# A hybrid SSD, pooling and top-4-of-32 MoE block: another order of the experts, and down weights stored in 8 KB runs

## Chip, cores and metric

One core of a Trainium2 chip. The metric is the device time of one launch in microseconds (us); the kernel before takes 1842.26 us (median of 3 runs, 1841.16 to 1846.85).

## What is computed

The reference is one decoder block on 512 tokens of width 1024: a Mamba-2 branch and a pooling branch, merged by gates, then a mixture of experts, all in float32. The change is in the experts alone:

```python
logits = xt @ w_router + b_router
top_val, top_idx = lax.top_k(logits, 4)          # 4 of 32 experts for each token
gate = softmax(top_val)
# every expert gets its own tokens, padded to a block of rows:
gu = xblk @ w_gu[e] + b_gu[e]                    # 1024 -> 2048
glu, lin = split(gu, 2)
glu = minimum(glu, 7.0); lin = clip(lin, -7.0, 7.0)
act = glu * sigmoid(1.702 * glu) * (lin + 1.0)
y = act @ w_down[e] + b_down[e]                  # 1024 -> 1024
# y * gate is added to the token's row
```

An expert's weights are 12 MB (8 MB up, 4 MB down), so 32 experts read 384 MB.

## The kernel before

**Ranks and blocks.** The kernel counts each expert's tokens on the chip and sorts the experts by that count. `ROOM` gives each rank a fixed number of slots: rank 0 (expert 0, always taken first) 128, ranks 1 to 15 64 (a *half* block), ranks 16 to 30 72 to 128 (a *whole* block), and rank 31, the largest expert, 192: a whole block and a half one with the same weights. `order_of_ranks` (L62) writes the order of the ranks down as a table; `order[u]` is the rank of the u-th unit of work, and `big` is the place of rank 31. In the table `s` draws the next half rank, `f` the next whole one, and `None` stands for rank 31. Before, the order is 0, 1, 2, then 16, 3, 17, 4, 18, 5, 19, 6, 20, 7, 31, 8, 21, 9, 22, 10, 23, 11, 24, 12, 25, 13, 26, 27, 28, 29, 30, 14, 15.

**A unit on TensorE.** The loop over u (L1358) does `up(u)`, then `down(u - 1)`, so that the activation of unit u runs beside the down projection of the unit before it. `up` starts with the bias rows (`bias_rows`: L1107 for a whole block, L1104 for a half one, output `mm`) and takes 8 pieces of 1 MB; `down` starts with bias rows too (output `ss`) and takes 4 pieces. The starts of these bias matmuls mark the stretches of the program in the trace. A whole block's weights are split in two halves of float32r parts by ScalarE (`wh`, L117) and VectorE (`wl`, L118), 1024 columns at a time and into two buffers, and each product is three matmuls (L1118 to L1120). A half block takes its weights straight from the loaded tile in float32 (L1113), without a split.

**Beside it.** `acts` (act_rows, L1154 to L1156, and act_turn, L1164 or L1167) makes the activation of unit u in hooks inside `down(u - 1)`. `turned(u + 1)` transposes and normalizes the next unit's tokens (L1066, L1074) in the same `down`. `send` scales the result (L1178) and GpSimd adds it to the output in DRAM.

**Weight loads.** All weight loads stand in one queue, SP's (`fetch`, L771), in the order in which they are used: 8 up pieces of unit u, then 4 down pieces of unit u - 1. They go round a ring of tiles of 1 MB (7 that come back, and 4 more after unit 0: 11 in all); a load waits until its tile's last reader is done.

Of the kernel before, what the change touches and what calls it, by code (L numbers as in the profile page):

```python
# [20 lines left out]
P = 128  # L21
D = 1024
# [4 lines left out]
NE = 32  # L27
# [33 lines left out]

def order_of_ranks():  # L62
    s, f = iter(range(FIXED, FIXED + SMALL)), iter(range(FIXED + SMALL, NE - 1))
    kinds = [s, s] + [f, s] * 5 + [None, s] + [f, s] * 5 + [f] * 5 + [s, s]
    return list(range(FIXED)) + [next(k) if k else NE - 1 for k in kinds]


# [1 line left out]
def hybrid_block(ctx: ExitStack, tc: tile.TileContext, cst, cols, rows, xt, xf, wad0, wada, bada,  # L69
                 wx, wz, wdt, wu, wg, wso, wpl, wpo, wo, wr, ball, wgu, wdn, out):  # L70
    nc = tc.nc
    V, S, G, TE, SP = nc.vector, nc.scalar, nc.gpsimd, nc.tensor, nc.sync
# [9 lines left out]
    def T_(tag, cols_, dt=F32, parts=P):  # L82
        if tag in shared:
            o = shared[tag]
            return Z[0:parts, o:o + cols_]
        uid[0] += 1
        return sb.tile([parts, cols_], dt, tag=tag, name=f"{tag}_{uid[0]}")
# [655 lines left out]
    def weights(e):  # L743
        def of(w, lo_, hi_):
            return w[e, lo_:hi_, :] if isinstance(e, int) else w[bass.ds(e, 1), lo_:hi_, :].squeeze(0)

        return dict(wu=lambda k: of(wgu, k * P, (k + 1) * P), got={},
                    wd=lambda c: of(wdn, c * 256, (c + 1) * 256).rearrange("(k p) d -> p k d", p=P))

    order = order_of_ranks()  # L750
    big = order.index(NE - 1)
    tab, wts, rk = {}, {}, {}

    def weights_of(u):
        if u not in wts:
            wts[u] = weights(order[u] if u < FIXED else
                             SP.value_load(rk["eidi"][0:1, order[u]:order[u] + 1], min_val=0, max_val=NE - 1))
        return wts[u]
# [6 lines left out]
    def fetch(w, kind, k, t=None):  # L765
        if t is None:
            t = ring.pop(0)
            if t not in ("S7", "r3", "S3"):
                ring.append(t)
        r = T_(t, 2048)  # L770
        SP.dma_start(r if kind == "wu" else r.rearrange("p (k d) -> p k d", k=2), w[kind](k))  # L771
        return r

    def eload(w, kind, k):
        return w["got"].pop((kind, k), None) or fetch(w, kind, k)
# [46 lines left out]
    def prefetch(i0, i1):  # L822
        w = weights_of(0)
        for k in range(i0, i1):
            w["got"]["wu", k] = fetch(w, "wu", k)

    def fetch_down(c0, c1):
        w = weights_of(0)
        for c in range(c0, c1):
            w["got"]["wd", c] = fetch(w, "wd", c, kept[c])  # L830
# [400 lines left out]
    def tabled(u):  # L1231
        ev = SP.value_load(tab["eui"][0:1, u], min_val=0, max_val=NE - 1)
        ec, ub, eo, pu, gvu, gvf = (T_(n, c, d) for n, c, d in (
            ("ec", 2, F32), ("ub", 1, F32), ("eo", NE, F32), ("pu", 4, F32), ("gvu", 12, BF16), ("gvf", 12, F32)))
        V.tensor_copy(ec[:, 0:1], tab["euf"][:, u])
        V.tensor_copy(ec[:, 1:2], tab["ruf"][:, u])
        V.tensor_copy(ub, tab["ubase"][:, u])
        V.tensor_scalar(eo, i32c, ec[:, 1:2], None, op0=ALU.is_equal)
        gvt = T_("q16", 512)
        pv = gvt[:, 0:P].rearrange("p (b e) -> p b e", b=NB)  # L1240
        tt(pv, rk["pos"], eo.unsqueeze(1).to_broadcast([P, NB, NE]), ALU.mult)
        V.tensor_reduce(pu, pv, axis=AX.X, op=ALU.add)
        V.tensor_scalar(pu, pu, ub, None, op0=ALU.subtract)
        gvx = gvt[:, P:P + 384].rearrange("p (b c e) -> p b c e", b=NB, c=3)
        for b in range(NB):
            tt(gvx[:, b], GVv[:, b].rearrange("p e c -> p c e"), eo.unsqueeze(1).to_broadcast([P, 3, NE]), ALU.mult)
        V.tensor_reduce(gvf.rearrange("p (b c) -> p b c", c=3), gvx, axis=AX.X, op=ALU.add)
        V.tensor_copy(gvu, gvf)
        eT = T_("eT", 2, F32R)
        sel_halves(eT, ec[:, 0:1])  # L1250
        return dict(pos=lambda b: pu[:, b:b + 1], gv=lambda b: gvu[:, b * 3:(b + 1) * 3], sel=dict(cols=eT), **weights(ev))
# [12 lines left out]
    def sel_of(u):  # L1264
        if u < FIXED:
            return dict(cols=sel0[:, 2 * u:2 * u + 2])
        return dict(cols=sels[u % 2], wide=wides[u % 2])
# [90 lines left out]
    for u in range(NE + 1):  # L1358
        hooks = {}
        if u < NE:  # L1360
            w, sel = weights_of(u), sel_of(u)
# [73 lines left out]
    with tc.For_i(0, nov, 1) as i:  # L1435
        lastp.clear()
        w = tabled(bass.ds(i, 1))
# [20 lines left out]
def _consts():  # L1458
    c = np.zeros((P, C_ALL), np.float32)
    i = np.arange(P)  # L1460
    c[:, C_ID:C_ID + P] = np.eye(P)
    c[:, C_TRI:C_TRI + P] = i[:, None] <= i[None, :]
    c[:, C_STRI:C_STRI + P] = i[:, None] < i[None, :]
    c[:, C_IOTA:C_IOTA + P + 1] = np.arange(P + 1)[None, :]
    c[:, C_E:C_E + 32] = (i[:, None] % 32) == np.arange(32)[None, :]
    for g in range(4):
        c[:, C_RC + g * 16:C_RC + (g + 1) * 16] = 1.0 / np.minimum(np.arange(16) + 1, 2 << g)
    c[:, C_P], c[:, C_NP] = i, -i
    c[:, C_P5] = i + 512
    c[:, C_PM:C_PM + 2] = (i % 32)[:, None]  # L1470
    c[:, C_B:C_B + 4] = np.arange(4) * P - 512
    key = np.arange(NE)
    key[:FIXED] -= 40000 * (FIXED - key[:FIXED])
    c[:, C_KR:C_KR + NE] = key
    c[:, C_KC] = key[i % 32]
    c[:, C_HM] = i < 64
    c[:, C_H] = i >= 64
    c[:, C_BD:C_BD + 4] = (i // 32)[:, None] == np.arange(4)
    c[:, C_CAP:C_CAP + NE] = [room(r) for r in range(NE)]
    return c  # L1480


def _layout(i):
    A = np.ascontiguousarray

    def tiles(w):
        return w.reshape(KD, P, w.shape[1] // P, P).transpose(2, 1, 0, 3)

    def pairs(t):
        return t.reshape(-1, 2, P, 1024).transpose(0, 2, 1, 3).reshape(-1, P, 2048)  # L1490

    def halves(w):
        n = w.shape[1] // 512
        return w.reshape(2, 4, P, n, 512).transpose(3, 0, 2, 1, 4).reshape(n, 2, P, 2048)

    x, w_in = i["x"][0], i["w_in"][0]
    fcol = lambda v: v.reshape(-1, P).T
    cols = np.concatenate([
        i["conv_w"][0].reshape(4, 24, P).transpose(2, 1, 0).reshape(P, 96), fcol(i["conv_b"][0]),
        fcol(i["ssd_norm_w"][0]), fcol(i["pool_scale"][0]), fcol(i["norm_mix_w"][0]), fcol(i["c"][0]),  # L1500
        fcol(i["norm_ffn_w"][0]), fcol(np.repeat(i["d_skip"][0], 64)),
        fcol(i["norm_final_w"]), fcol(i["b_ada"][0][:2048]).reshape(P, 2, 4, 2).transpose(0, 2, 1, 3).reshape(P, 16)], axis=1)
    rows = np.concatenate([i["a_log"][0], i["dt_bias"][0], i["b_router"][0]])
    order = [t for g in range(4) for t in (16 + g, 20 + g, 4 * g, 4 * g + 1, 4 * g + 2, 4 * g + 3)]
    d = dict(
        cst=_consts(), cols=A(cols), rows=rows,
        xt=A(x), xf=A(x.T.reshape(2, 4, P, T).transpose(0, 2, 1, 3).reshape(2, P, 2048)),
        wad0=A(i["w_ada"][0][:, :2048].reshape(2, 4, P, 2, 4, 256).transpose(4, 0, 2, 1, 3, 5).reshape(4, 2, P, 2048)), wada=A(halves(i["w_ada"][0][:, 2048:])), bada=A(i["b_ada"][0].reshape(12, 512)),
        wx=A(pairs(tiles(w_in[:, 2048:5120])[order])),
        wz=A(pairs(tiles(w_in[:, 0:2048]))),  # L1510
        wdt=A(w_in[:, 5120:5152].reshape(KD, P, NH).transpose(1, 0, 2).reshape(P, 256)),
        wu=A(pairs(tiles(w_in[:, 5152:6176]))),
        wg=A(pairs(tiles(w_in[:, 6176:8224]))),
        wso=A(i["w_ssd_out"][0].reshape(4, 4, P, 2, 4, P).transpose(0, 3, 2, 4, 1, 5).reshape(8, P, 2048)),
        wpl=A(i["w_pool"][0].reshape(4, 2, P, 256).transpose(2, 0, 1, 3).reshape(P, 2048)),
        wpo=A(pairs(tiles(i["w_pool_out"][0]))),
        wo=A(halves(i["w_out"][0]).reshape(4, P, 2048)),
        wr=A(i["w_router"][0].reshape(KD, P, NE).transpose(1, 0, 2).reshape(P, 256)),
        ball=A(np.concatenate([i["b_gu"][0], i["b_down"][0]], axis=1).reshape(NE, 3, 2, 512).transpose(2, 0, 1, 3).reshape(2, NE, 1536)),
        wgu=A(i["w_gu"][0]), wdn=A(i["w_down"][0]))  # L1520
    return d


# [17 lines left out]
```

## Time and profile before

| | us |
|---|---|
| median of 3 runs | 1842.26 (1841.16 to 1846.85) |
| the profiled execution | 1837.33 |
| its span, first to last instruction | 1835.5 |

TensorE's matmuls are busy 1754.0 us (96% of the span), VectorE 1210.0 (66%), ScalarE 947.1 (52%), GpSimd 237.5 (13%). The experts fill the second part of the span, from about 709 us on. The chain that ended last is of no use here: it is cut after its last instruction. So the kernel is read by stretches: which engine's idle time ends with whom, and how long a unit takes beside which neighbours.

### The profile page before, as it was taken

How to read it: one execution, taken by the hardware profiler on the slowest of the kernel's cores; microseconds unless marked ns; L12 is line 12 of the kernel's file. 1: busy time of each engine (PE TensorE's matmuls, PEld its weight loads, DVE VectorE, ACT ScalarE, POOL GpSimd, SP SyncE). 2: the span in 40 equal slices, each digit the busy share in tenths (PEclk: the TensorE clock that was granted, in tenths of full speed). 3: DMA queues.
4: the chain of work that ended last, by engine and by line, in shares of the span. 5: the costliest groups of instructions: out<-in, count | busy, mean ns of one | idle time of the engine just before them, and what ended most of it. 6: DMA issues, size and time to landing. Idle time of an engine off the chain costs nothing. (4 is left out here: it accounts for less than half of the span.)

```text
span 1835.5 us, 23325 instructions
## 1 busy us (share of the span) xinstructions
PE 1754.0 (96%) x8352; PEld 1161.8 (63%) x8353; DVE 1210.0 (66%) x1803; ACT 947.1 (52%) x1458; POOL 237.5 (13%) x214
## 2 busy tenths in 40 slices
PE   6999999999999999999999999999999999999995
PEld 3777687777778877455566465455564565677741
DVE  5888685858564558666576565375675585799933
ACT  4533554537362346355455455264555465677833
POOL 0000001010000002112111111121212112212111
PEclk8999999999999999999999999999999999999998
DMA  9265334253444368899999999789999999999894
GB/s 355 75 241 218 115 115 138 83 137 103 116 115 183 127 226 321 324 403 396 413 402 394 407 404 352 289 331 374 396 402 394 402 402 365 405 360 342 313 370 192
DMA packets 102728, 527.81 MB, mean 288 GB/s; under 512 B 11737, under 2 KB 12377, under 8 KB 60368
## 3 DMA queue, kind: packets, MB, share of 16 engines
q1 hardware_dynamic: 90544, 498.14, 69.7%
q0 software_dynamic: 11184, 25.50, 6.4%
q10 hardware_dynamic: 880, 2.64, 0.4%
q8 instruction: 67, 1.10, 0.2%
q14 instruction: 53, 0.43, 0.1%
HBM read 502.89 MB, written 25.77 MB: 288 GB/s over the span
## 5 line engine op out<-in xcount | busy, mean ns | idle before, releaser
L118 DVE TENSOR_TENSOR wl<-r,wh 128x1024 fp32r<-128x1024 f32 x246 | 301.3, 1252 | 105.0 <-ACT wh L117 87.0
L117 ACT ACTIVATE wh<-r 128x1024 fp32r<-128x1024 f32 x246 | 254.0, 1057 | 133.0 <-PE mm L266 56.3
L118 DVE TENSOR_TENSOR wl<-S,wh 128x1024 fp32r<-128x1024 f32 x186 | 229.3, 1268 | 32.8 <-ACT wh L117 32.2
L1119 PE MATMUL mm<-wl,S 128*128 128x512 f32 x540 | 214.2, 397 | 8.0 <-DVE wl L118 7.7
L117 ACT ACTIVATE wh<-S 128x1024 fp32r<-128x1024 f32 x186 | 190.0, 1056 | 54.0 <-PE mm L1120 30.2
L1120 PE MATMUL mm<-wh,S 128*128 128x512 f32 x540 | 213.0, 394 | 0.0
L265 PE MATMUL mm<-S,wh 128*128 128x512 f32 x512 | 206.5, 404 | 3.9 <-ACT S L117 3.9
L267 PE MATMUL mm<-S,wl 128*128 128x512 f32 x512 | 205.1, 401 | 1.5 <-DVE wl L118 1.5
L266 PE MATMUL mm<-S,wh 128*128 128x512 f32 x512 | 205.5, 401 | 0.0
L1118 PE MATMUL mm<-wh,S 128*128 128x512 f32 x540 | 182.1, 400 | 1.9 <-ACT wh L117 1.4
L1154 DVE TENSOR_SCALAR q<-mm 128x512 f32<-128x512 f32 x49 | 33.5, 688 | 151.9 <-PE mm L1113 124.6
L1155 ACT ACTIVATE q<-q 128x512 f32<-128x512 f32 x50 | 31.5, 632 | 192.2 <-DVE q L1154 192.0
L1118 PEld LDWEIGHTS mm<-wh,S 128*128 128x128 f32 x540 | 101.1, 188 | 39.3 <-issue 9.7
L1119 PEld LDWEIGHTS mm<-wl,S 128*128 128x128 f32 x540 | 101.3, 188 | 37.2 <-DVE wl L118 14.2
L265 PEld LDWEIGHTS mm<-S,wh 128*128 128x128 f32 x512 | 96.4, 188 | 32.8 <-issue 6.8
L1120 PEld LDWEIGHTS mm<-wh,S 128*128 128x128 f32 x540 | 101.4, 188 | 21.8
L267 PEld LDWEIGHTS mm<-S,wl 128*128 128x128 f32 x512 | 96.3, 188 | 29.5 <-issue 6.6
L266 PEld LDWEIGHTS mm<-S,wh 128*128 128x128 f32 x512 | 96.5, 188 | 26.6 <-issue 4.2
L1119 PE MATMUL ss<-wl,S 128*128 128x512 f32 x240 | 98.8, 412 | 3.1 <-DVE wl L118 3.1
L1120 PE MATMUL ss<-wh,S 128*128 128x512 f32 x240 | 94.8, 395 | 0.0
L1113 PE MATMUL mm<-S,S 128*64 128x512 f32 x408 | 94.5, 595 | 0.0
L1179 POOL TENSOR_TENSOR y<-y,q 128x512 f32<-128x512 f32 x47 | 63.7, 1367 | 209.7 <-ACT y L1178 209.7
(498 smaller groups left out, 3086.9 us busy)
## 6 DMA issues: line engine op xcount, KB each, us to landing
S<-in_wgu SPq DMA_DIRECT2D x113, 1024.0 KB, 12.1
r<-in_wgu SPq DMA_DIRECT2D x97, 1024.0 KB, 10.1
S<-in_wdn SPq DMA_DIRECT2D x61, 1024.0 KB, 12.7
r<-in_wdn SPq DMA_DIRECT2D x44, 1024.0 KB, 14.9
bc<-in_wgu SPq DMA_DIRECT2D x23, 1024.0 KB, 11.3
Z<-in_wgu SPq DMA_DIRECT2D x23, 1024.0 KB, 10.1
r<-in_wada SPq DMA_DIRECT2D x16, 1024.0 KB, 6.0
r<-in_wx SPq DMA_DIRECT2D x12, 1024.0 KB, 6.2
```

The lines of the kernel that those rows point to most:

```text
L117: S.activation(hi, src, AF.Copy)
L118: V.tensor_tensor(lo, src, hi.bitcast(F32), op=ALU.subtract)
L265: TE.matmul(ps, a, hh(k), start=k == 0, stop=False)
L266: TE.matmul(ps, a, hl(k), start=False, stop=False)
L267: TE.matmul(ps, b, hh(k), start=False, stop=k == KD - 1)
L1113: lastp[:] = [TE.matmul(rows_of(ps, n0 + i), x.c[k], hl[:, o + i * 512:o + (i + 1) * 512], start=False, stop=stop).ins]
L1118: TE.matmul(p, x.h[k], h, start=False, stop=False)
L1119: TE.matmul(p, x.h[k], l, start=False, stop=False)
L1120: lastp[:] = [TE.matmul(p, x.l[k], h, start=False, stop=stop).ins]
L1154: V.tensor_scalar(g, pg, LIM, None, op0=ALU.min)
L1155: S.activation(t, g, AF.Tanh, scale=ALPHA / 2)
L1179: G.tensor_tensor(yn, yn, gaf2[0] if half else gaf[n], op=ALU.mult)
```

## The change

The table of the order is another one, and the down weights are laid out on the host so that two rows of one partition's piece lie together: a piece of 1 MB is 128 runs of 8 KB where it was 256 of 4 KB. The bytes, the tiles and the instructions of a unit stay.

```diff
 def order_of_ranks():
     s, f = iter(range(FIXED, FIXED + SMALL)), iter(range(FIXED + SMALL, NE - 1))
-    kinds = [s, s] + [f, s] * 5 + [None, s] + [f, s] * 5 + [f] * 5 + [s, s]
+    kinds = [s, s] + [f, f, s] * 3 + [s, None, s, s] + [f, f, s] * 3 + [f, s] * 3 + [s]
     return list(range(FIXED)) + [next(k) if k else NE - 1 for k in kinds]
...
-                    wd=lambda c: of(wdn, c * 256, (c + 1) * 256).rearrange("(k p) d -> p k d", p=P))
+                    wd=lambda c: of(wdn, c * P, (c + 1) * P))
...
-        SP.dma_start(r if kind == "wu" else r.rearrange("p (k d) -> p k d", k=2), w[kind](k))
+        SP.dma_start(r, w[kind](k))
...
-        wgu=A(i["w_gu"][0]), wdn=A(i["w_down"][0]))
+        wgu=A(i["w_gu"][0]), wdn=A(i["w_down"][0].reshape(NE, 4, 2, P, D).transpose(0, 1, 3, 2, 4)).reshape(NE, 4 * P, 2 * D))
```

The order of the ranks is now 0, 1, 2, then 16, 17, 3, 18, 19, 4, 20, 21, 5, 6, 31, 7, 8, 22, 23, 9, 24, 25, 10, 26, 27, 11, 28, 12, 29, 13, 30, 14, 15.

What it moves in the instructions, on ScalarE first, where the second of two whole blocks begins. (`q<-mm` with `colf` and the `S<-q` behind it are the second whole block's tokens, the `y` row scales the half block's result, and `wh` is the first split of the second whole block's weights.) Before, from the one place where a whole block came after a half one and was followed by another whole one (ranks 26 and 27):

```order
L1167 ACTIVATE S_1583_11584<-ss_11601 128x512
L1167 ACTIVATE S_1583_11584<-ss_11623 128x512
L1074 ACTIVATE q_1597_11637<-mm_11638,colf_388 128x128 x4
L117 ACTIVATE S_1596_11636<-q_1597_11637 128x512
L1074 ACTIVATE q_1599_11649<-mm_11650,colf_388 128x128 x4
L117 ACTIVATE S_1596_11636<-q_1599_11649 128x512
L1178 ACTIVATE y_11667<-ss_11585,gate_1475_10743 128x512
L117 ACTIVATE wh_713_5236<-S_1607_11690 128x1024 x2
```

After, in a group of two whole blocks and a half one behind the largest expert:

```order
L1167 ACTIVATE S_1395_10309<-ss_10326 128x512
L1167 ACTIVATE S_1395_10309<-ss_10348 128x512
L1074 ACTIVATE q_1409_10362<-mm_10363,colf_388 128x128 x4
L117 ACTIVATE S_1408_10361<-q_1409_10362 128x512
L1074 ACTIVATE q_1411_10374<-mm_10375,colf_388 128x128 x4
L117 ACTIVATE S_1408_10361<-q_1411_10374 128x512
L1178 ACTIVATE y_10392<-ss_10310,gate_1283_9367 128x512
L117 ACTIVATE wh_713_5236<-r_1419_10415 128x1024 x2
```

The piece is the same; it stood once before and stands six times after.

On VectorE, where the first of two whole blocks goes down while the second one's activation is made and a half block comes next (`q<-mm` L1154 and L1156: the clips that begin the two activations, `wl` the splits for the down projection). Before, ranks 29, 30 and 14:

```order
L1154 TENSOR_SCALAR q_1738_12877<-mm_12673 128x512
L1154 TENSOR_SCALAR q_1743_12913<-mm_12674 128x512
L118 TENSOR_TENSOR wl_715_5238<-S_1737_12859,wh_713_5236 128x1024 x2
L1156 TENSOR_SCALAR q_1740_12879<-mm_12675 128x512
L111 SCALAR_TENSOR_TENSOR q_1739_12878<-q_1739_12878,q_1738_12877 128x512
L118 TENSOR_TENSOR wl_714_5237<-S_1742_12895,wh_712_5235 128x1024
L111 SCALAR_TENSOR_TENSOR q_1740_12879<-q_1740_12879,q_1739_12878 128x512
L118 TENSOR_TENSOR wl_714_5237<-S_1742_12895,wh_712_5235 128x1024
L1156 TENSOR_SCALAR q_1745_12915<-mm_12676 128x512
```

After, in the first group behind the largest expert:

```order
L1154 TENSOR_SCALAR q_1436_10610<-mm_10407 128x512
L1156 TENSOR_SCALAR q_1438_10612<-mm_10409 128x512
L118 TENSOR_TENSOR wl_715_5238<-S_1435_10592,wh_713_5236 128x1024 x2
L111 SCALAR_TENSOR_TENSOR q_1437_10611<-q_1437_10611,q_1436_10610 128x512
L118 TENSOR_TENSOR wl_714_5237<-r_1440_10628,wh_712_5235 128x1024
L111 SCALAR_TENSOR_TENSOR q_1438_10612<-q_1438_10612,q_1437_10611 128x512
L118 TENSOR_TENSOR wl_714_5237<-r_1440_10628,wh_712_5235 128x1024
L1154 TENSOR_SCALAR q_1441_10646<-mm_10408 128x512
L1156 TENSOR_SCALAR q_1443_10648<-mm_10410 128x512
```

The second activation's first clip (L1154) has moved behind the four splits; the number of each kind is the same.

## Rows read from the trace of the kernel before

**Rows 1.** The page: busy time and share of the span of TensorE with the number of its matmuls, and the slices of the span (40 equal ones) with the busy share of the DMA engines in tenths and what they moved in GB/s.

```profile
PE 1754.0 (96%) x8352; PEld 1161.8 (63%) x8353; DVE 1210.0 (66%) x1803; ACT 947.1 (52%) x1458; POOL 237.5 (13%) x214
...
DMA  9265334253444368899999999789999999999894
GB/s 355 75 241 218 115 115 138 83 137 103 116 115 183 127 226 321 324 403 396 413 402 394 407 404 352 289 331 374 396 402 394 402 402 365 405 360 342 313 370 192
```

**Rows 2.** Busy us of each engine (and instructions) in four stretches of the experts: two pairs of a whole and a half block, then the end of the run of whole blocks, then the two half blocks behind it. Columns: the stretch, its length, PE, PEld, DVE, ACT, POOL, granted TensorE clock, DMA share, GB/s.

```profile
925.00:991.00 66.00, 63.13 (x298) 38.12 (x297) 42.10 (x57) 36.03 (x51) 11.74 (x10) 1.00 1.02 402
991.00:1057.00 66.00, 63.16 (x309) 37.99 (x308) 42.37 (x66) 36.16 (x51) 12.81 (x11) 1.00 1.02 406
...
1585.00:1747.00 162.00, 152.44 (x703) 118.89 (x702) 149.55 (x166) 125.81 (x161) 41.23 (x19) 1.00 0.92 345
1747.00:1800.00 53.00, 50.91 (x229) 22.16 (x228) 16.94 (x27) 14.91 (x24) 8.83 (x7) 1.00 1.02 385
```

**Rows 3.** Who ended TensorE's idle time from 793 to 1777 us, from the start of unit 3 to that of unit 31: us in total, times, longest. These are all the causes but one of 0.2 us.

```profile
PE ss L1066 <- DVE q L111: 19.1, 13, 1.6
PE mm L1119 <- DVE wl L118: 7.7, 12, 0.8
PE ss L1059 <- DVE ixs L114: 5.5, 9, 1.5
PE ss L1119 <- DVE wl L118: 5.4, 9, 1.6
PE mm L1118 <- ACT wh L117: 1.4, 2, 1.2
```

**Rows 4.** What SP's queue of weight loads (L771) waited for from 860 to 1585 us, the two longest: us in total, times, longest.

```profile
SPq L771 <- DVE wl L118: 239.8, 106, 6.1
SPq L771 <- PE ss L1113: 149.8, 44, 5.0
```

**Rows 5.** TensorE in order of time (start us, us, engine, line, operation): the bias matmuls that begin, in a pair, the whole block's up, the earlier half block's down, the next half block's up, the whole block's down, and the next whole block's up.

```profile
925.22 1.09 PE L1107 MATMUL mm<-bt,sel 128*128 128x512 f32 x4
...
949.70 0.39 PE L1104 MATMUL ss<-bt,sw 128*128 128x512 f32 x1
...
961.27 0.74 PE L1104 MATMUL mm<-bt,sw 128*128 128x512 f32 x2
...
976.70 0.74 PE L1107 MATMUL ss<-bt,sel 128*128 128x512 f32 x2
...
991.35 1.09 PE L1107 MATMUL mm<-bt,sel 128*128 128x512 f32 x4
```

**Rows 6.** The same in the run of whole blocks: the starts of the ups (`mm`) of ranks 26, 27, 28, 30 and 14, and of the downs (`ss`) of ranks 26 and 29.

```profile
1549.47 1.09 PE L1107 MATMUL mm<-bt,sel 128*128 128x512 f32 x4
...
1585.25 1.19 PE L1107 MATMUL mm<-bt,sel 128*128 128x512 f32 x4
...
1611.51 0.63 PE L1107 MATMUL ss<-bt,sel 128*128 128x512 f32 x2
...
1627.80 1.09 PE L1107 MATMUL mm<-bt,sel 128*128 128x512 f32 x4
...
1707.85 1.09 PE L1107 MATMUL mm<-bt,sel 128*128 128x512 f32 x4
...
1731.84 0.63 PE L1107 MATMUL ss<-bt,sel 128*128 128x512 f32 x2
...
1746.85 0.62 PE L1104 MATMUL mm<-bt,sw 128*128 128x512 f32 x2
```

**Rows 7.** The same for half blocks beside each other: the starts of the ups of ranks 2 (behind rank 1) and 16, and of rank 15 (behind rank 14).

```profile
768.04 0.62 PE L1104 MATMUL mm<-bt,sw 128*128 128x512 f32 x2
...
793.02 0.95 PE L1107 MATMUL mm<-bt,sel 128*128 128x512 f32 x3
...
1777.14 0.62 PE L1104 MATMUL mm<-bt,sw 128*128 128x512 f32 x2
```

**Rows 8.** The same around the largest expert: the starts of the ups of ranks 7, 31, 8 and 21.

```profile
1093.91 0.74 PE L1104 MATMUL mm<-bt,sw 128*128 128x512 f32 x2
...
1124.38 1.09 PE L1107 MATMUL mm<-bt,sel 128*128 128x512 f32 x4
...
1178.63 0.73 PE L1104 MATMUL mm<-bt,sw 128*128 128x512 f32 x2
...
1218.70 1.20 PE L1107 MATMUL mm<-bt,sel 128*128 128x512 f32 x4
```

**Rows 9.** ScalarE in order of time at the start of rank 27's up: the last conversion of rank 27's tokens, the scaling of rank 13's result, the first splits of rank 27's weights.

```profile
1585.54 0.63 ACT L117 ACTIVATE S<-q 128x512 fp32r<-128x512 f32 x1
1586.08 0.67 ACT L1178 ACTIVATE y<-ss,gate 128x512 f32<-128x512 f32 x1
1586.65 3.89 ACT L117 ACTIVATE wh<-S 128x1024 fp32r<-128x1024 f32 x4
```

**Rows 10.** The page's DMA issues, up and down pieces into the same kind of tile: times, KB each, median us from issue to landing.

```profile
r<-in_wgu SPq DMA_DIRECT2D x97, 1024.0 KB, 10.1
...
r<-in_wdn SPq DMA_DIRECT2D x44, 1024.0 KB, 14.9
```

## The prediction

> **What bounds the kernel now.** I read the page first, then the stretch of the experts, and there the waits. On the page TensorE is busy 96% of the span, and in the experts' part the DMA engines stand at nine tenths or more in most slices with around 400 GB/s [rows 1]. So two things could set the pace, and the reader should see that a busy share settles nothing. The stretches say the same more sharply: in a pair of a whole and a half block (66 us) TensorE is busy 63.1 us and the DMA share is 1.02 [rows 2]. What settles it is who ends TensorE's idle time. Of some 39 us between 793 and 1777 us, all is put down to VectorE and ScalarE, nothing to a load [rows 3]; and the queue of loads itself waits for VectorE's splits and TensorE's matmuls to give a tile back [rows 4]. The loads are nearly full, but they are ahead; TensorE, with the short waits for its splits and activations, sets the pace. The clock is at 1.00 in all these stretches [rows 2], its level of 2.4 GHz.
>
> Order can then matter only through what stands beside a unit. So I price a unit by its neighbours: the time from the start of its up to the start of the next one's, which holds its own up and the down of the unit before it. I write w for whole, h for half, B for the largest, and the middle letter is the unit priced.
>
> - hwh 961.27 - 925.22 = 36.05; whw 991.35 - 961.27 = 30.08 [rows 5].
> - hww 1585.25 - 1549.47 = 35.78; the three www 1707.85 - 1585.25 = 122.60, of which the first is 1627.80 - 1585.25 = 42.55; wwh 1746.85 - 1707.85 = 39.00; whh 1777.14 - 1746.85 = 30.29 [rows 6, 7].
> - hhw 793.02 - 768.04 = 24.98 [rows 7].
> - whB 30.47, hBh 54.25, Bhw 40.07 [rows 8].
>
> **The change, part by part.** By the two tables of ranks, units 3 to 30 were 10 hwh, 9 whw, 1 whB, 1 hBh, 1 Bhw, 1 hww, 3 www, 1 wwh, 1 whh. Now they are 3 hwh, 7 whw, 6 hww, 6 wwh, 2 whh, 1 hhB, 1 hBh, 1 Bhh, 1 hhw. The units before and behind stand as they stood.
>
> Removed: 7 hwh (252.4), 2 whw (60.2), whB (30.5), Bhw (40.1), 3 www (122.6) and the old wwh (39.0): 544.8 us.
>
> Added: 5 hww at 35.78, 178.9. Six wwh: this is the term that decides. The only wwh of before came at the end of a run, with its splits already flowing. The new ones are second of two, and such a block begins late. ScalarE first converts its tokens and scales the half block's result, and only then, 1.4 us after the up has begun, makes the first split (1586.65 against 1585.25) [rows 6, 9]. That up took 1611.51 - 1585.25 = 26.26 us [rows 6] against 24.48 in a pair [rows 5]. The instruction order of the change has the same ScalarE piece at the new places, so I take the late up each time. The down of the first block, beside the second one's activation and in front of a half block, is the 1746.85 - 1731.84 = 15.01 us behind rank 29 [rows 6]; on VectorE one clip has moved behind four splits there, with as many instructions, which I cost at nothing: the splits come at most one clip later or earlier. So a new wwh is 26.26 + 15.01 = 41.27, six are 247.6. Its bounds are the old wwh (39.00) and the first www (42.55), nearest is the sum of its own two parts.
>
> Further 1 whh (30.3), hhw (25.0), hhB, which I take as hhw since a half block's up and down are the same (25.0; the bound above is whB, 30.5), and Bhh as Bhw (40.1). Added in all: 178.9 + 247.6 + 30.3 + 25.0 + 25.0 + 40.1 = 546.9. **Sum: +2.1 us.**
>
> The down weights in runs of 8 KB: the same 128 loads of 1 MB from the same queue, with half as many packets. The nearest rows are the up pieces, whose rows are 8 KB already: 10.1 us from issue to landing where a down piece takes 14.9 [rows 10]. If all of the 4.8 us were due to the runs, a down piece would land 4.8 us earlier; no engine waits for it [rows 3], so I cost it at nothing. The cover is the loads' lead; without it, all of the 4.8 us at one load per unit, 32 of them, would be 154 us, far more than the 39 us that TensorE idles at all. A loss has no row. The Trainium skill, Perfetto Trace Analysis, section DMA Optimizations, says that fewer and larger pieces (2 KB to 4 KB or 8 KB) can improve throughput dramatically when a kernel is bound by DMA; here the waits put that condition out of force, and by the rule the sum would be that of the second rival below.
>
> GpSimd's gathers, scatters and selections are the same in number and only change places; no wait of TensorE names them [rows 3]. The SP queue has the same loads in the new order.
>
> The profiled execution takes 1837.33 us with a span of 1835.5, so it would become 1839.4; the median of the runs stands 4.9 us above it, and I carry the difference over: 1842.26 + 2.1 = **1844.4 us**.
>
> **The rivals.**
>
> *The late start doesn't recur.* If the second whole block's splits come in time at the new places, each wwh costs the old 39.00, 2.27 less, and six give 13.6: 1844.4 - 13.6 = 1830.8. For it: one place alone shows the late start [rows 9]. Against it: the order of instructions is the same there. Chance 0.11.
>
> *The loads set the pace of the pairs after all.* Then TensorE's idle time in a pair, 66 - 63.1 = 2.9 us [rows 2], is a consequence of the loads, and a group of two whole blocks and a half one, with 36 MB in 107 us, is free of it: six groups, 17.4 us, 1827.0. For it: the DMA share of 1.02. Against it: rows 3 name no load, and rows 4 have the loads waiting for the engines. The Trainium skill, Perfetto Trace Analysis, section Roofline, gives about 435 GB/s as the ceiling of a core that runs alone; the 402 to 406 of the pairs are just under it, which is why I keep this rival. Chance 0.08.
>
> *Slower: half blocks side by side run out of weights.* Two half blocks in a row draw 24 MB, 25.2 million bytes, in 30.3 + 25.0 = 55.3 us; at the 402 GB/s of a pair they need 62.6 [rows 2, 6, 7]. That is 7.3 us short, at two new places on either side of the largest expert: 14.6 us, 1859.0. It decides if less than 2.9 MB, three of the ring's eleven tiles, are loaded ahead when the first half block begins. Against it: at the end of the program the same meeting, after whole blocks and at a DMA share of 1.02 [rows 2], leaves TensorE only 2.1 us idle of 53, and none of it by a load before 1777 [rows 3]. Both new places come behind whole blocks, in whose run the DMA share was 0.92 [rows 2], so the ring is full there. Chance 0.09.
>
> *Slower: the groups cost like the start of the run.* If VectorE can't keep up and every wwh costs the 42.55 of the first www, six add 7.7: 1852.1. In the run VectorE was busy 149.6 of 162 us [rows 2]; in a group the half block gives it time to catch up. Chance 0.08.
>
> **How the numbers follow.** The forecast holds 0.64, the rivals 0.36. The range takes in most of the first rival's and all of the fourth's result: 1832 to 1852. A measurement of this kernel can tell about 0.3% from no change, 5.5 us. The forecast's +2.1 lies inside; faster comes from the first two rivals, 0.19; slower from the last two, 0.17; within, 0.64.
>
> **What would show it.** Right: in the new profile the up of a second whole block takes about 26 us and begins with a wait for ScalarE's split, a wwh about 41, the pairs that remain 66; TensorE's waits name VectorE and ScalarE alone; the DMA share falls under 1.0 in the groups, with no effect. Wrong: pairs clearly under 66 us (the loads did count), ups of 24 us in the groups, or TensorE waiting for a load beside the largest expert.

## The result, and the profile after

| | before | after |
|---|---|---|
| median of 5 runs each, side by side | 1843.28 us (1841.16 to 1849.05) | 1858.94 us (1856.04 to 1861.54) |
| ratio | | 1.0091, 95% interval 1.007 to 1.0112 |
| the profiled execution, its span | 1837.33 us, 1835.5 us | 1859.25 us, 1857.5 us |
| unit 3's up to unit 31's up | 984.1 us | 1001.1 us |

The change makes the kernel slower by 15.7 us; forecast were +2.1 and a range that ended at 1852. In the profiled executions 17.0 us stand between unit 3 and unit 31. Another 5.7 us are gone before the experts begin (714.9 us against 709.2). They don't belong to the change: a kernel with the same order and layout (the later activation, below) begins its experts at 708.5 us. From 414.7 to 425.0 us this one execution of the changed kernel has TensorE at 0.50 of its clock, the profiled one of before has 1.00 there (fourth row of the fence on the clock, below); that this is all of the 5.7 us is not shown.

The page of the changed kernel: TensorE, the DMA engines in 40 slices, the packets, and one of the down loads. It answers to [rows 1, 10].

```profile
PE 1770.5 (95%) x8353; PEld 1165.8 (63%) x8353; DVE 1210.5 (65%) x1803; ACT 944.7 (51%) x1458; POOL 233.2 (13%) x214
...
DMA  8265233352444368899999999799999898999995
...
DMA packets 86345, 527.81 MB, mean 284 GB/s; under 512 B 11738, under 2 KB 12378, under 8 KB 27601
...
r<-in_wdn SPq DMA_DIRECT2D x44, 1024.0 KB, 7.2
```

TensorE's busy time has grown by 16.5 us with the same matmuls, part of it before the experts: a hint to look for matmuls that got slower, not only for idle time. Down pieces into a tile `r` land in 7.2 us where they took 14.9. The mean rate over the span is lower than before, because the span is longer.

Who ended TensorE's idle time from 798 to 1800 us in the changed kernel (us in total, times, longest), against [rows 3]:

```profile
PE ss L1066 <- DVE q L111: 14.7, 10, 1.6
PE ss L1119 <- DVE wl L118: 11.1, 7, 1.8
PE mm L1118 <- ACT wh L117: 8.2, 13, 1.2
PE mm L1119 <- DVE wl L118: 7.6, 12, 0.8
PE ss L1059 <- DVE ixs L114: 1.5, 3, 0.5
```

No load stands here, as before. Two rows have grown: the waits of an up for ScalarE's split (1.4 to 8.2 us) and those of a down for VectorE's (5.4 to 11.1). Others shrank, so that the five rows together rose by only 4.0 us (39.1 to 43.1). Most of the 17.0 us is therefore not seen as idle time.

TensorE in order of time in one group behind the largest expert (start us, us, line): the starts of the first whole block's up, of the earlier half block's down, the second whole block's up, the first one's down, the half block's up, the second one's down, and the next group. It answers to [rows 5, 6].

```profile
1382.47 1.09 PE L1107 MATMUL mm<-bt,sel 128*128 128x512 f32 x4
...
1406.94 0.39 PE L1104 MATMUL ss<-bt,sw 128*128 128x512 f32 x1
...
1418.26 1.19 PE L1107 MATMUL mm<-bt,sel 128*128 128x512 f32 x4
...
1444.54 0.63 PE L1107 MATMUL ss<-bt,sel 128*128 128x512 f32 x2
...
1460.32 0.62 PE L1104 MATMUL mm<-bt,sw 128*128 128x512 f32 x2
...
1476.57 0.73 PE L1107 MATMUL ss<-bt,sel 128*128 128x512 f32 x2
...
1491.25 1.09 PE L1107 MATMUL mm<-bt,sel 128*128 128x512 f32 x4
```

So hww is 1418.26 - 1382.47 = 35.79 (forecast 35.78), wwh 26.28 + 15.78 = 42.06 (forecast 26.26 + 15.01), whw 16.25 + 14.68 = 30.93 (forecast 30.08). All units of the changed kernel, read in the same way:

| unit | count | forecast, each | measured, each | together against the forecast |
|---|---|---|---|---|
| hww | 6 | 35.78 | 35.7 | -0.5 |
| wwh | 6 | 41.27 | 40.1, 44.7, 42.1, 42.1, 42.1, 44.5 | +8.0 |
| whw behind two whole blocks | 5 | 30.08 | 30.9 | +4.2 |
| hhB, hBh, Bhh, hhw | 1 each | 25.0, 54.25, 40.1, 25.0 | 24.8, 56.3, 40.9, 27.2 | +4.8 |
| all others | | | | -1.7 |

The sum, 14.9 us before rounding, is what separates the measured 17.0 from the forecast 2.1.

Inside that group, the start of the second whole block's up on ScalarE, against [rows 9]:

```profile
1418.54 0.63 ACT L117 ACTIVATE S<-q 128x512 fp32r<-128x512 f32 x1
1419.08 0.67 ACT L1178 ACTIVATE y<-ss,gate 128x512 f32<-128x512 f32 x1
1419.65 1.99 ACT L117 ACTIVATE wh<-r 128x1024 fp32r<-128x1024 f32 x2
```

The first split begins at 1419.65, 1.39 us into the up, as forecast, and TensorE waits 1.21 us for it. The list of the change said that this piece stands six times; in the trace it stands five times. In the very first group a split runs before the last conversion and the scaling, 0.8 us ahead of the up (832.82), and the up takes 24.4 us:

```profile
832.01 1.07 ACT L117 ACTIVATE wh<-S 128x1024 fp32r<-128x1024 f32 x1
```

The down of the first block, on VectorE: the second activation's clips (L1154, L1156), products (L111), and splits (L118).

```profile
1450.67 0.69 DVE L1154 TENSOR_SCALAR q<-mm 128x512 f32<-128x512 f32 x1
1451.27 0.68 DVE L1156 TENSOR_SCALAR q<-mm 128x512 f32<-128x512 f32 x1
1451.87 0.68 DVE L111 SCALAR_TENSOR_TENSOR r<-ss,r 128x512 fp32r<-128x512 f32 x1
1452.47 0.68 DVE L111 SCALAR_TENSOR_TENSOR q<-q,q 128x512 f32<-128x512 f32 x1
1453.07 1.22 DVE L118 TENSOR_TENSOR wl<-r,wh 128x1024 fp32r<-128x1024 f32 x1
```

And TensorE, which needs that split; the second line is the same place of the kernel before, in the down from which the forecast took its 15.01 us:

```profile
1454.34 0.50 PE L1119 MATMUL ss<-wl,S 128*128 128x512 f32 x1 [1.77 <-DVE wl L118]
...
1741.15 0.50 PE L1119 MATMUL ss<-wl,r 128*128 128x512 f32 x1 [1.55 <-DVE wl L118]
```

Four operations, 0.6 us from start to start, stand in front of the split at 1453.07. The clip at 1450.67 is the one that the prediction moved at no cost. But the priced down held such a wait already, so the wait is only 0.22 us longer. Of the 0.77 us between 15.01 and 15.78, 0.27 stand before it: the first split of the down begins at 1444.89, 0.35 us into the down, behind a clip (L1156) that waits for the up's last product, where before it began at 1731.39, 0.45 us ahead of the down; TensorE's first matmul with it starts 1.62 us into the down instead of 1.18. The last 0.28 us stand behind the wait, where the eight small matmuls for a later unit's slots (L1038 and L1039, the *scores* below) have come into this down.

Last the clock: busy us in short stretches of the changed kernel around the two falls of the second group, and before the experts; the eighth column is the granted clock.

```profile
941.00:943.80 2.80, 1.41 (x4) 0.60 (x4) 2.80 (x7) 2.80 (x4) 2.24 (x2) 1.00 1.00 410
943.80:947.20 3.40, 2.86 (x8) 2.23 (x8) 3.40 (x4) 1.86 (x3) 0.71 (x1) 0.50 0.94 169
947.20:951.00 3.80, 3.80 (x18) 3.08 (x17) 3.12 (x4) 2.73 (x4) 0.00 (x0) 1.00 0.78 251
414.70:425.00 10.30, 8.89 (x18) 5.09 (x18) 6.80 (x11) 4.78 (x13) 0.54 (x1) 0.50 0.63 149
...
978.00:981.40 3.40, 3.40 (x11) 2.72 (x10) 3.40 (x4) 0.60 (x1) 0.00 (x0) 0.51 0.50 154
```

At 943.80 the clock goes to 0.50 (1.2 GHz) for 3.4 us, inside a late up, just after TensorE was busy for 1.41 of 2.80 us; at 978.00 again, in a down, just after a wait of 1.78 us. The matmuls of such a stretch count as busy: those from 945 to 946.7 us start 0.43 us apart, those in full clock 0.23. That is where busy time grew. There are four such falls in the groups (943.8, 978.0, 1530.9, 1565.0) and none between unit 3 and unit 31 in the profiled execution of before.

### The profile page after: what moved, and what is told of

Same layout as the page of the kernel before. It is cut to its first block, busy times and chain, and to the rows that moved or that the text cites. A ratio compares the mean times of both kernels' runs of the same rounds, so it can differ in the third digit from the quotient of the medians.

```text
span 1857.5 us, 23314 instructions
## 1 busy us (share of the span) xinstructions
PE 1770.5 (95%) x8353; PEld 1165.8 (63%) x8353; DVE 1210.5 (65%) x1803; ACT 944.7 (51%) x1458; POOL 233.2 (13%) x214
## 2 busy tenths in 40 slices
DMA packets 86345, 527.81 MB, mean 284 GB/s; under 512 B 11738, under 2 KB 12378, under 8 KB 27601
## 5 line engine op out<-in xcount | busy, mean ns | idle before, releaser
L118 DVE TENSOR_TENSOR wl<-r,wh 128x1024 fp32r<-128x1024 f32 x248 | 298.2, 1231 | 104.5 <-ACT wh L117 87.3
L117 ACT ACTIVATE wh<-r 128x1024 fp32r<-128x1024 f32 x248 | 255.1, 1056 | 128.8 <-PE mm L266 56.3
L118 DVE TENSOR_TENSOR wl<-S,wh 128x1024 fp32r<-128x1024 f32 x182 | 219.1, 1241 | 36.1 <-ACT wh L117 36.1
L1120 PE MATMUL mm<-wh,S 128*128 128x512 f32 x540 | 213.7, 397 | 0.0
L117 ACT ACTIVATE wh<-S 128x1024 fp32r<-128x1024 f32 x182 | 185.0, 1058 | 56.0 <-PE mm L1120 36.5
L1118 PE MATMUL mm<-wh,S 128*128 128x512 f32 x540 | 169.3, 402 | 8.5 <-ACT wh L117 8.2
L1119 PEld LDWEIGHTS mm<-wl,S 128*128 128x128 f32 x540 | 102.2, 189 | 39.1 <-DVE wl L118 16.0
L1154 DVE TENSOR_SCALAR q<-mm 128x512 f32<-128x512 f32 x49 | 33.7, 688 | 112.2 <-PE mm L1113 83.4
L118 DVE TENSOR_TENSOR S<-q,S 128x512 fp32r<-128x512 f32 x34 | 23.5, 691 | 97.2 <-ACT S L117 97.2
L1074 ACT ACTIVATE q<-mm,colf 128x128 f32<-128x128 f32 x132 | 49.7, 459 | 69.2 <-PE mm L1066 57.7
L1052 POOL DMA_INDIRECT S<-h_d,idx x31 | 51.8, 1670 | 234.7 <-PE ss L1120 102.6
## 6 DMA issues: line engine op xcount, KB each, us to landing
S<-in_wdn SPq DMA_DIRECT2D x61, 1024.0 KB, 11.4
```

What stands on the lines that cost most here:

```text
L117: S.activation(hi, src, AF.Copy)
L118: V.tensor_tensor(lo, src, hi.bitcast(F32), op=ALU.subtract)
L1052: G.indirect_dma_start(xe[0:n_, :], None, src, bass.IndirectOffsetOnAxis(ap=idx[0:n_, :], axis=0), bounds_check=lim, oob_is_err=False)
L1074: S.activation(out_[:, o], pt[:, o], AF.Identity, scale=colf[:, 8 + f:9 + f], bias=colf[:, f:f + 1])
L1118: TE.matmul(p, x.h[k], h, start=False, stop=False)
L1119: TE.matmul(p, x.h[k], l, start=False, stop=False)
```

## The experiments

Of each kernel the text below gives the ratio to the kernel before, run side by side with it (median 1843.78 in the first four, 1844.14 in the last four), and the length from unit 3's up to unit 31's of its profile: 984.1 before, 1001.1 after.

**The order alone.** The changed kernel with the old down layout (one of its three lines):

```diff
-                    wd=lambda c: of(wdn, c * P, (c + 1) * P))
+                    wd=lambda c: of(wdn, c * 256, (c + 1) * 256).rearrange("(k p) d -> p k d", p=P))
...
```

> The new order with the old layout of the down weights. Theory A (the order alone costs the time, in the groups: the second whole block, the half block behind it, and TensorE's clock falling there): about +15 us against the kernel before, 1856 to 1861 us, with the same stretches as the changed kernel (second whole block 42 us, half block behind it 30.9 us) and falls of the clock inside the groups. Theory B (the 8 KB runs move the loads and with them the rest): within 5 us of the kernel before.

1860.69 us, ratio 1.0087 (1.0062 to 1.0111); unit 3 to 31 1004.1. Every kind of unit has the same length as in the changed kernel, except where a clock fall lies in it. The order is the whole loss, as far as the noise tells.

**The layout alone.** The kernel before with the new down layout (the same lines the other way round).

> The old order with the down weights in 8 KB runs. Theory A: no change, within 3 us of the kernel before, pairs at 66.1 us, since no engine waits for a load. Theory B: about 10 to 15 us slower. If the loads did set the pace of the pairs: up to 17 us faster, with TensorE's 2.9 us of idle time in a pair gone.

1843.48 us, ratio 1.0 (0.9986 to 1.0013); unit 3 to 31 984.9. Its page has 86345 packets, the kernel before 102728. The down pieces on its page and, below, on that of the order alone:

```profile
r<-in_wdn SPq DMA_DIRECT2D x44, 1024.0 KB, 13.8
...
r<-in_wdn SPq DMA_DIRECT2D x44, 1024.0 KB, 5.6
```

16,383 packets fewer, and no time: nobody waits for these loads. So the condition in the rule that the prediction took from the Trainium skill (Perfetto Trace Analysis, section DMA Optimizations), that the kernel is bound by DMA, was rightly read as not met. In the old order the pieces still take 13.8 us, and with the new order and the old layout 5.6: the 7.2 us of the changed kernel come with its order.

**Groups alone**, four of them, single half blocks around the largest expert, old layout:

```diff
-    kinds = [s, s] + [f, s] * 5 + [None, s] + [f, s] * 5 + [f] * 5 + [s, s]
+    kinds = [s, s] + [f, f, s] * 2 + [f, s] * 3 + [None, s] + [f, f, s] * 2 + [f, s] * 3 + [f] + [s, s]
```

> Old layout; four groups of two whole blocks and a half one and no run of whole blocks, single half blocks around the largest expert as before. By the forecast's prices (second whole block 41.3 us, half block behind it 30.1): +2.6 us. By theory A with the prices of the changed kernel (42.1 and 30.9): +9 us, and 2 to 5 us more if the clock falls in the groups. If the cost lies around the largest expert: within 3 us of the kernel before.

1854.08 us, ratio 1.0053 (1.0034 to 1.0072); unit 3 to 31 994.3, which is +10.2. The four wwh took 40.1, 43.7, 43.7 and 44.5, the whw behind them 30.9 each.

**Two half blocks on either side of the largest expert alone**, pairs and the run of whole blocks kept, old layout:

```diff
-    kinds = [s, s] + [f, s] * 5 + [None, s] + [f, s] * 5 + [f] * 5 + [s, s]
+    kinds = [s, s] + [f, s] * 5 + [s, None, s, s] + [f, s] * 3 + [f] * 7 + [s, s]
```

> Old layout; pairs as before, two half blocks on either side of the largest expert, and the two whole blocks that this frees put into the run at the end (seven of them there). By the forecast's prices: -2.3 us. By theory A with the prices of the changed kernel (half block between a half and a whole one 27.2, largest 56.3): +2.5 us. If half blocks beside each other run out of weights: +10 us or more, with waits for a load beside the largest expert.

1846.37 us, ratio 1.0007 (0.9992 to 1.0023); unit 3 to 31 988.1, +4.0. hhB 24.8, hBh 56.3, Bhh 40.9, hhw 27.2, all as in the changed kernel, and TensorE waits for no load. The median can't be told from no change; the cost is read from these units. So the half blocks don't run out of weights: the 1859.0 us of that rival is the measured time, but its mechanism doesn't occur. A number that fits is no proof of a cause. The two parts add up: against the forecast's prices four groups cost 7.6 us too much (10.2 instead of 2.6) and the middle 6.3 (4.0 instead of -2.3); six groups and the middle, 11.4 + 6.3 = 17.7, are an estimate for the order alone, which measured 17.9 (20.0 instead of 2.1).

**The first split of a whole block earlier**, in the changed kernel. The up's first piece is split while the down before it still runs:

```diff
+    def split_early(u):
+        w = weights_of(u)
+        w["got"]["wu", 0] = fetch(w, "wu", 0)
+        ahead.append(list(pieces(w["got"]["wu", 0], True)))
...
+            if prev is not None and u + 1 < NE and room(order[u + 1]) > 64:
+                c = 1 if room(order[u - 1]) <= 64 else 3
+                hooks[c] = [lambda: split_early(u + 1)] + hooks.get(c, [])
```

> The changed kernel, with the first up piece of a whole block split while the down before it still runs: behind the down's second piece where that down is a half block's, behind its fourth where it is a whole block's. Nothing else is edited. Theory A (a whole block whose up follows a half block's down begins late, because ScalarE's first split stands behind its conversions and scaled results, and the wait sometimes takes TensorE's clock down with it): the up of the second whole block falls from 26.3 us to about 24.5 in four groups of six, in the two groups with a clock fall from 27.4 and 27.1 to 24.5, and the largest expert's up from 45.3 to about 43.3, together 3 x 1.8 + 2.9 + 2.6 + 2.0 = about 13 us, less where a clock fall stays: unit 3's up to unit 31's about 988 instead of 1001.1, a time of 1845 to 1850, ratio 0.992 to 0.995 to the changed kernel. Theory B (the late start is only where TensorE happens to wait, and the wait moves to the next piece, since VectorE and ScalarE lack the time in a group): the ups stay at 26 or more and the time at 1857 to 1861.

1839.83 us, ratio 0.9976 (0.9959 to 0.9993); unit 3 to 31 982.6, 18.5 less than the changed kernel and more than the 13 that were expected. The second whole blocks give 10.9 of it; the first ones (3.9) and the three pairs that remain (4.1) gain too, which was not expected. Its waits from 790 to 1800 us, and the starts of the same group's second up, its down and the half block's up:

```profile
PE ss L1066 <- DVE q L111: 15.7, 10, 1.7
PE ss L1119 <- DVE wl L118: 11.1, 7, 1.8
PE ss L1059 <- DVE ixs L114: 5.4, 8, 0.8
PE mm L1107 <- ACT q L1074: 3.3, 5, 0.7
PE mm L1119 <- DVE wl L118: 1.1, 5, 0.2
PE ss L1113 <- DMA r<-in_wdn: 0.2, 1, 0.2
```

```profile
1407.67 0.96 PE L1107 MATMUL mm<-bt,sel 128*128 128x512 f32 x3
1409.28 0.50 PE L1107 MATMUL mm<-bt,sel 128*128 128x512 f32 x1 [0.65 <-ACT q L1074]
...
1432.27 0.63 PE L1107 MATMUL ss<-bt,sel 128*128 128x512 f32 x2
...
1448.04 0.62 PE L1104 MATMUL mm<-bt,sw 128*128 128x512 f32 x2
```

The 8.2 us behind ScalarE's first split are gone, and 6.5 of the 7.6 behind the first `wl`. The up takes 24.60 us instead of 26.28, and the first of a group, which never waited for long, 23.2 instead of 24.5. What is late next is seen in two rows: a bank of `mm`, the matmuls' output, that ScalarE's normalizing (L1074) gives back 0.65 us late, and VectorE's `ixs`. A load is named for the first time, with 0.2 us. Not everything gains: the half block behind Bhh (hhw) takes 29.8 us instead of 27.2, with a wait of 1.69 us and a fall of the clock in its down. The down is 15.77 us as before, its waits too.

**The second activation one piece later** in the first block's down, in the changed kernel:

```diff
-            hooks = {n: [f] for n, f in enumerate(acts(pss[0], aTs[0]))}
+            late1 = prev is not None and u < NE - 1 and room(order[u]) > 64 and room(order[u - 1]) > 64 and room(order[u + 1]) <= 64
+            hooks = {n + late1: [f] for n, f in enumerate(acts(pss[0], aTs[0]))}
```

> The changed kernel, with the activation of the second whole block of a group begun one piece later in the down of the first (behind its second and third piece instead of its first and second). Nothing else is edited. Theory A (VectorE's clips and products in front of the down's splits make TensorE wait, 1.8 us in one place, which the prediction costed at nothing): the down of the first whole block falls from 15.8 us to about 15.0, and the clock falls that stood in that down (978.0, 1565.0) don't come back: 6 x 0.8 = 4.8 us, up to 8 with the clock, of which the scores of the next unit, which move into the half block's up, may take back 1: a time of 1852 to 1856. Theory B (the clips are hidden, the longer down comes from the matmuls that stand between): no change, 1857 to 1861.

1855.49 us, ratio 1.0063 (1.0046 to 1.008), whose interval overlaps that of the changed kernel. The median lies in the range of theory A, but unit 3 to 31 takes 1001.1 us, no gain, so that hit says nothing. The waits of the downs, and the starts of a group's first down, its half block's up and the second down:

```profile
PE ss L1119 <- DVE wl L118: 6.6, 7, 1.0
```

```profile
1439.67 0.63 PE L1107 MATMUL ss<-bt,sel 128*128 128x512 f32 x2
...
1454.62 0.63 PE L1104 MATMUL mm<-bt,sw 128*128 128x512 f32 x2
...
1472.16 0.73 PE L1107 MATMUL ss<-bt,sel 128*128 128x512 f32 x2
```

The down falls to 14.95 us, its wait to 1.02. That this is close to the 15.01 that had been forecast is chance, since the priced down waits 1.55 us. The edit does two things at once: it moves the clips and products, which shortens the wait by 0.75 us, and it moves the scores out of the down. So it shows that VectorE's order sets this wait, and doesn't price the one clip. The half block's up behind it grows from 16.25 to 17.54 us. TensorE in that up, first in the changed kernel, then with the edit:

```profile
1462.92 1.94 PE L1113 MATMUL mm<-bc,S 128*64 128x512 f32 x8
1464.69 1.89 PE L1113 MATMUL mm<-S,S 128*64 128x512 f32 x8
1466.51 0.55 PE L1066 MATMUL mm<-cst,S 128*128 128x128 f32 x3
...
1457.33 1.07 PE L1113 MATMUL mm<-bc,S 128*64 128x512 f32 x2
1458.34 0.25 PE L1059 MATMUL ss<-GV,wrt 128*128 128x3 bf16 x4
1458.52 1.50 PE L1113 MATMUL mm<-bc,S 128*64 128x512 f32 x5
1459.44 0.59 PE L1113 MATMUL mm<-S,S 128*64 128x512 f32 x1
...
1462.10 0.88 PE L1066 MATMUL mm<-cst,S 128*128 128x128 f32 x6
```

A half block's matmuls run in pairs: two of them start within 0.01 us, and the next two 0.43 us later, so that eight take 1.77 us. With the edit the scores stand in front of the first row of the second part (0.28 us from 1457.05 on), and four of the sixteen matmuls start alone, two of them at 1457.33 and 1457.81, each taking as long as a pair. The sixteen last 4.6 us instead of 3.6, at a granted clock of 1.00. That makes 1.3 us; the transposes (six and two instead of three and five) take 1.17 us either way. Why the partners come apart is not shown. Six times 0.8 won, six times 1.3 lost there (5 whw, 1 whh); the rest of the balance is two clock falls fewer. The direction of the first was expected; the size of the second was not.

**Both edits.**

> Both edits in the changed kernel: first up pieces of whole blocks split early, and the second whole block's activation one piece later in the first one's down. Theory A (two sets of waits that the new neighbours bring, which add): 13 + 4 = about 17 us off the changed kernel, 1841 to 1846, so the same as the kernel before; unit 3's up to unit 31's 983 to 988. Theory B (groups cost what they cost, whatever stands first): 1855 to 1861.

1838.76 us, ratio 0.9973 (0.9958 to 0.9988); unit 3 to 31 981.8. The gains of the early split stand, those of the second edit go to the half blocks' ups again (17.5 each). TensorE waits 0.8 us for loads here.

**The early split in the kernel before**, the control.

> The kernel before, with the same early split as a control: the first up piece of a whole block is split while the down before it still runs. In the pairs the down before a whole block's up is a whole block's, and the order of TensorE's work stays the same there. Theory A: only the start of the run of whole blocks (rank 27, up of 26.26 us) gains, 2 us at most: 1838 to 1844, which can't be told from no change. Theory B (early splits help every whole block, so that the gain in the groups has nothing to do with what stands before them): 0.8 us at each of 12 pairs and more, 10 us off, 1833 or less.

1827.78 us, ratio 0.9906 (0.9888 to 0.9923); unit 3 to 31 971.2. It beats both kernels, and here my expectation of 2 us failed: the gain is 16 us. The whole block's up of a pair, against [rows 5]:

```profile
927.83 1.09 PE L1107 MATMUL mm<-bt,sel 128*128 128x512 f32 x4
...
951.00 0.39 PE L1104 MATMUL ss<-bt,sw 128*128 128x512 f32 x1
```

23.17 us instead of 24.48. The old pairs began late too, by less: a wait of 0.76 us for the first `wl` at 929.47 and slower matmuls around it. I had called [rows 3] waits that set the pace and then priced all the pairs as a fixed 66 us. About 1.3 us in each of eight pairs, 0.7 in hww and 1.7 in the first www make 12.6 of the 12.9 us that are gone between unit 3 and unit 31. The medians differ by more, 16.4 us; the mean granted clock of these runs was 0.9928 against 0.9907 and, as an estimate, 0.0021 of 1840 us is 3.9 us, about the rest. So early splits don't belong to the groups; they help every whole block, most where it is late by most. Between the two kernels with early splits the order still costs 11.4 us (982.6 against 971.2): the first blocks' downs (15.8 us), the half blocks behind them (30.9), three clock falls and the units around the largest expert stand there as they did. The late start alone does not explain the loss.

## Why the prediction was wrong

- *TensorE sets the pace, loads are ahead; the 8 KB runs cost nothing*: right. No row of waits names a load in the kernels before and after (0.2 and 0.8 us are named where the early split stands in the new order), and the layout alone gives 1.0 (0.9986 to 1.0013).
- *hww 35.78, and the late up of the second block, 26.26*: right, 35.7 and 26.3. In the very first group it doesn't occur (24.4), 1.9 us the other way: the order on ScalarE is another there.
- *The clip on VectorE "which I cost at nothing: the splits come at most one clip later or earlier"*: **this step failed.** The down takes 15.78 us, not 15.01, six times 0.77 or 4.6 us. About 0.5 of each 0.77 is VectorE's order: the down's first split begins later (0.27), and clips and products in front of a later split lengthen a wait (1.77 instead of 1.55). The other 0.28 is the scores on TensorE, which the row of the forecast didn't hold. This division is read from the rows; no run separates it. The numbers of instructions were the same; their place was not.
- *"The clock is at 1.00 in all these stretches"* was carried over without a term: **this step failed too.** The four falls lengthen the wwh by about 5.0 us (ups of 27.4 and 27.1 instead of 26.3, two downs of 17.3 instead of 15.8). The mean granted clock is 0.9902 over 24 runs of before and 0.9876 over the five of after. As an estimate, if TensorE is the bound while its clock is down, the lost time is that share of the run: 18.1 us of 1843.8 before, 23.1 of 1858.9 after, so about 5 of the 15 us. The profiled execution of before had 0.993, which goes with the 4.9 us that it stood below the median.
- *whw 30.08 wherever it stands*: **wrong** behind two whole blocks, 30.9, five times, 4.2 us in all; its up takes 16.25 us instead of 15.42, without a wait. In [rows 5] its matmuls run behind all eight transposes in one piece. In the changed kernel the transposes and the four small matmuls of the gates (L1059) cut the pairs three times. At each cut the last pair takes 0.53 us and the next one 0.48 instead of 0.43, 0.45 us in all; the gates take 0.18 and the transposes in two pieces 0.2 more.
- *hhB, Bhh and hBh like their nearest neighbours*: hhB 24.8 was right; the others were **mis-sized** by 5.0 us together. The largest expert's up takes 45.3 us instead of 43.3, without a wait: of its 64 half-block matmuls 8 start alone, where before all ran in pairs, and four pairs' time more is 1.7 us. With the early split 4 start alone, and it takes 44.3. So a late first split is at most part of it. The hhw was priced from rank 2, whose up (14.77 us) holds neither scores nor transposes; behind the largest expert the up holds both, 4 matmuls start alone, and it takes 17.3. The 2.2 us of hhw and 0.8 of Bhh recur in the kernel with that change alone; the early split brings Bhh back to 39.7.
- *The rivals.* That the late start doesn't recur, that loads set the pace, and that half blocks run out of weights are all refuted (the first holds in one group of six). That a wwh costs the 42.55 of the run's first www was the best price: measured 42.6 on average. Its reason, VectorE behind, was part of it (the downs), the clock another. Even with it the sum would have been 1852, since whw and the middle were priced from other neighbours.

The clock falls and the waits go together in the profiles. Of 18 late ups (those of the groups behind the first in the changed kernel, with the order alone, with the groups alone, and with the later activation) 10 hold a fall (one of these ten, behind the largest expert with the groups alone, after three waits of only 0.4 to 0.5 us), of the 12 ups with early splits none. Of 22 downs with the 1.8 us wait 7 hold one, of the 12 where the wait is 1.0 us none. That waits of this length bring the clock down is thus likely. It isn't shown as a rule: the pairs' waits for the activation's product (13 in [rows 3], 1.6 us at most) hold none, and a wait of 1.69 us for the same product, in the hhw of both kernels with early splits in the new order, is followed by one each time.

## What to carry to other kernels

Price a unit by everything that stands beside it, two neighbours back, and by the piece of each engine's order, not by the number of instructions in it: an operation that has moved in front of a producer is a wait. Where TensorE is the bound, read a pattern that recurs (here the first wait of every whole block) as a cost to remove before reordering around it; in the old order that was worth 16 us, while the new order lost 15.7. And take one term for the clock: new waits of a microsecond or two may cost more than they last.

## What the runs showed of the hardware

- TensorE's granted clock falls to 0.50 for 3.4 us (once 6.8, in the kernel with the order alone) in the middle of a stretch at 1.00, after waits of 1.2 to 1.8 us in some places; a unit with one 3.4 us fall was 0.8 to 1.6 us longer than its like. The spread of the runs goes with it: the kernel before took 1838.43 us at a mean clock of 0.994 and 1848.71 at 0.988.
- Small matmuls between the long ones of a half block are dear beyond their own length. The long ones (128*64) run in pairs, 0.43 us from pair to pair; at each cut the pairs on either side took 0.15 us more together, and matmuls that lost their partner took a pair's time each. The scores moved into a half block's up start 25 ns apart and last 0.28 us; the up took 1.3 us longer.
